# Gate tiles of the SwiGLUs in pairs: seven block products in place of eight

## The chip, the cores and the metric

The kernel runs on one core of one Trainium2 chip. The metric is the device time of one execution in microseconds. Five engines work side by side, each on its own queue of instructions: TensorE (matmuls, PE in the profile, with its weight loads shown apart as PEld), VectorE (DVE), ScalarE (ACT), GpSimd (POOL) and SyncE (SP), which issues most of the DMA transfers. A time is the slowest core's, and here there is one core.

## The reference

Two layers of an encoder act on 512 tokens of width 1024. A layer is a SwiGLU, a mixer (two attentions, a pooling branch, gates, an output map) and a second SwiGLU, each behind an RMS norm with shift and scale, each added to x under a gate. Shift, scale and gate come from a vector c through `w_ada`. The change touches the SwiGLU alone, of which the program runs four:

```
def swiglu(h, w_gate, w_up, w_down):
    return (jax.nn.silu(h @ w_gate) * (h @ w_up)) @ w_down
...
h = modulate(rms_norm(x, norm_gain[l, 0]), mod[:, 0], mod[:, 1])
x = x + 0.5 * mod[:, 2][:, None, :] * swiglu(h, ffn_w_gate[l, 0], ffn_w_up[l, 0], ffn_w_down[l, 0])
```

`w_gate` and `w_up` are 1024 x 2816, `w_down` is 2816 x 1024, all in float32.

## The kernel before

**Layout.** Features lie on the 128 partitions, tokens along the free dimension. The normed input h is held as eight blocks of 128 channels x 512 tokens. 2816 hidden features are 22 tiles of 128.

**Precision.** A float32 matmul is made of three matmuls in the faster type float32r. Each operand is split into a high half, the value rounded to float32r by ScalarE, and a low half, the rest, by VectorE (`split_to`, line 369; for weights `wchunk`, lines 268 and 270). `triple` (lines 117 to 122) issues high x high, high x low and low x high into one PSUM accumulation. So h lives in SBUF as `hhi` and `hlo`, and every weight block that comes from DRAM costs one ScalarE cast (L268) and one VectorE subtraction (L270).

**A SwiGLU** (`Ffn.run`, line 461). The 22 tiles are worked in two parts, of 12 and 10. For each tile, `gate_up` loads the gate and the up weights (512 KB each, eight blocks of 128 x 128), `unit` runs 8 x 3 matmuls of 512 columns for each into a PSUM bank, and `act` (line 452) makes silu of the gate on ScalarE (L454), the product on VectorE (L456) and its two halves (L370, L371). When the tiles of a part are done, `k_outer` (line 374) runs the down projection over this part's tiles: chunks of two tiles x 512 output channels, first for channels 0 to 511, then for the others. The first chunks are used as they come; the last two, or three, are held so that each of four output tiles ends by itself. `residual_tail` (line 416, L420) adds each output tile to x. The last part's second half is worked by halves of 256 tokens, so that the next phase's norm can begin on the first half.

**The beginning of a SwiGLU.** The very first one starts from `start` (line 523), which works three tiles while the norm is made. The others take tiles 0 and 1 by halves of the tokens behind the two halves of the norm (`Norm.back_start`, L357 to L360: scale, high half with shift, low half).

**Modulation rows.** The 144 rows of `w_ada` (512 KB each) are loaded and reduced on VectorE (`mod_step`, L194 and L197) as a side work: in the SwiGLUs each weight chunk adds `MOD_RATE`, here 1.0, to a credit, and each whole credit is one row. Rows go into the tag "v2", which has four buffers, as long as a SwiGLU is not in its last down stage.

**Buffers.** Tags of the SBUF pool that matter here, each a set of equal buffers that its tiles share: "b" with 17 blocks of 128 x 1024 (the products of a part, two halves each in one block), "v2" with 4, "raw" with 2 (weights as loaded), "whi" and "wlo" with 3 each, "ptb" with 2 (double size), "strip" with 2. In PSUM, "acc" and "mm" have four banks each; a bank holds 128 x 512.

**Order.** The program text is in the order of priority, and the Tile layer sets each engine's order of instructions from it: an instruction whose buffer or operand is not due yet can be passed by later ones of its engine. On the chip each engine works its list in order. Work off TensorE's path is placed by `later(delay, fn)` (line 98): it runs once the planned TensorE time, counted in 512-column matmuls in `pe[0]`, has gone on by `delay`. `issue_after` keeps some instructions behind others by hand, such as a modulation row's load behind the last weight load.

Of the kernel before, what the change touches and what calls it, by code (L numbers as in the profile page):

```python
# [15 lines left out]
F32 = mybir.dt.float32  # L16
F32R = mybir.dt.float32r
# [23 lines left out]
def encoder_kernel(tc, xT, c, w_ada, b_ada, gains, w_gate, w_up, w_down, w_qkv, w_f, w_ubg,  # L41
# [72 lines left out]
            t.run()  # L114
        polling[0] = False

    def triple(o, lh, ll, rh, rl, start, stop):
        poll()
        mm(o, lh, rh, start=start, stop=False)  # L119
        mm(o, lh, rl, start=False, stop=False)  # L120
        mm(o, ll, rh, start=False, stop=stop)  # L121
        pe[0] += 3.0 * max(o.shape[-1], 256) / T


# [98 lines left out]
        while mod_ptr[0] < min(len(mod_queue), (l * 9 + j + 1) * 8 - 16):  # L223
            mod_pop()

    MOD_RATE = 1.0
    in_ffn = [True]
    lo_share = [0, 0]

# [10 lines left out]
        else:  # L240
            yield

    def wchunk(src, shape, side=True, spare=None, lo_eng=None):
        if lo_eng is None:
            lo_share[1] += 1
            lo_eng = nc.gpsimd if lo_share[0] and lo_share[1] % lo_share[0] == 0 else nc.vector
        if quiet[0] > 0:
            quiet[0] -= 1
            if quiet[0] == 0:
                gate.clear()  # L250
        elif side and in_ffn[0] and mod_tag[0] == "v2":
            mod_credit[0] += MOD_RATE
            while mod_credit[0] >= 1.0:
                mod_credit[0] -= 1.0
                mod_pop()
        raw = st([P] + list(shape), F32, *(("b", NB) if spare else ("raw", NRAW)))
        last["dma"] = nc.sync.dma_start(raw, src).ins
        if spare == "ptb":
            both = st([P, 2] + list(shape), F32R, "ptb", 2)
            hi, lo = both[:, 0], both[:, 1]  # L260
        elif spare == "b":
            hi = st([P] + list(shape), F32R, "b", NB)
            lo = st([P] + list(shape), F32R, "b", NB)
        else:
            hi = st([P] + list(shape), F32R, "whi", 3)
            lo = st([P] + list(shape), F32R, "wlo", 3)
        with behind("scalar"):
            nc.scalar.copy(hi, raw)  # L268
        with behind("vector"):
            lo_eng.tensor_tensor(lo, raw, hi.bitcast(F32), op=ALU.subtract)  # L270
        return hi, lo
# [22 lines left out]
    class Norm:  # L294


        def __init__(self, l, s, xtag):
            self.l, self.s, self.xtag = l, s, xtag
            self.ssum = st([P, T], F32, "ssum", 1)
            self.xa = [None] * 4  # L300
            self.work = [None, None]
            self.state = [0, 0]
            self.pieces = [[], []]

        def sq(self, d, hs):

# [37 lines left out]
        def back_start(self, hs, bank):  # L344
            if self.state[hs] > 1:
                return
            self.front(hs, bank)
            self.state[hs] = 2
            w = self.work[hs]
            rb = bank((P, HALF))  # L350
            mm(rb, ones, w[:, HALF:2 * HALF], start=True, stop=True)  # L351
            cols = slice(hs * HALF, (hs + 1) * HALF)

            def piece(d):
                b = modc[:, self.l, 3 * self.s, d:d + 1]
                t = self.xa[d // 2][:, d % 2, cols]
                nc.vector.tensor_tensor(t, rb, t, op=ALU.mult)  # L357
                hi = hhi[:, d, cols]
                a_ins = nc.scalar.activation(hi, t, AF.Identity, bias=b)
                v_ins = nc.vector.scalar_tensor_tensor(hlo[:, d, cols], t, b, hi.bitcast(F32),  # L360
                                                       op0=ALU.add, op1=ALU.subtract)
                gate["scalar"], gate["vector"] = a_ins.ins, v_ins.ins
                last["norm"] = v_ins.ins

            self.pieces[hs] = [lambda d=d: piece(d) for d in range(KD)]
# [5 lines left out]
        lo_eng.tensor_tensor(lo, src, hi.bitcast(F32), op=ALU.subtract)  # L371


    def k_outer(chunk_src, nch, lhs_rhs, before_last=None):

        if before_last is None:
            parts, nheld = [(None, slice(0, T), [acc() for _ in range(4)])], 2
# [12 lines left out]

        held = []
        for c in range(nch):
            if before_last is not None:
                if c == nch - 2:
                    quiet[0] = 8
                    before_last()
                quiet[0] = 8
            hi, lo = wchunk(chunk_src(c), (2, T))  # L400
            if c < nch - nheld:
                for part in parts:
                    for j in range(4):
                        go(part, j, [(c, hi, lo)])
            else:
                held.append((c, hi, lo))
        if before_last is not None:
# [19 lines left out]
    FRONT, BACK, FRONT1, BACK1 = 8, 24, 16, 28  # L427
    FRONT2, BACK2 = 16, 28
    STEP = 3


    class Ffn:
# [19 lines left out]
        def act(self, n, pg, pu):  # L452
            sg = t1(T)
            nc.scalar.activation(sg, pg, AF.Silu)  # L454
            pr = t2(T)
            nc.vector.tensor_tensor(pr, pu, sg, op=ALU.mult)  # L456
            a = blk("b")
            split_to(a[:, 0, :], a[:, 1, :], pr)
            return a

        def run(self, nxt):
            l, s, ms = self.l, self.s, self.ms
            in_ffn[0] = True
            mod_tag[0] = "v2"
            for part, (f0, nf) in enumerate(((0, 12), (12, 10))):
                acts = []
                n = 0
                if part == 0 and self.norm is None:
                    acts = self.start()
                    n = 3  # L470
                elif part == 0:
                    g0, u0, g1 = self.pre
                    pg, pu, pg1 = mmt(), mmt(), mmt()
                    for hs in range(2):
# [14 lines left out]
                    n = 2  # L489
# [8 lines left out]
                mod_need(l, 3 * ms + 2)  # L498
                for c0 in (0, T):
# [8 lines left out]
                    last = part == 1  # L508
# [4 lines left out]
                    hook = None  # L513
                    if split:
                        hook = nxt.prefetch_weights if nxt is not None else (lambda: None)
                    for j, hs, o in k_outer(src, nf // 2, ops, hook):
                        d = c0 // P + j
                        residual_tail(d, hs, o, modc[:, l, 3 * ms + 2, d:d + 1], nxt if last else None)
                        if last and nxt is None:
                            cols = slice(0, T) if hs is None else slice(hs * HALF, (hs + 1) * HALF)  # L520
                            nc.sync.dma_start(out[:, d, cols], xd(d)[:, cols])

        def start(self):

# [566 lines left out]
```

## Time and profile before

| | us |
|---|---|
| median of 3 runs | 2472.27 (2471.41 to 2472.57) |
| the profiled execution | 2472.68 |
| its span in the profile | 2470.9 |

| engine | busy us | share of the span | instructions |
|---|---|---|---|
| TensorE matmuls (PE) | 2424.9 | 98% | 11898 |
| TensorE weight loads (PEld) | 2028.9 | 82% | 11898 |
| VectorE (DVE) | 1328.2 | 54% | 2362 |
| ScalarE (ACT) | 981.6 | 40% | 1634 |
| GpSimd (POOL) | 377.3 | 15% | 439 |

The page gives busy time by engine, the span in slices, the chain of work that ended last, the costliest groups of instructions and the DMA issues. Groups name the line of the kernel, the engine, the operation and its tiles, then the busy time, the mean of one in ns, and the idle time ahead of them with what ended it. Matmuls overlap in the records: one of 512 columns is recorded with 389 ns, but the next starts well before that has passed. So the price of a matmul is read from the distance of starts, not from its record.

The SwiGLUs lie at about 0 to 385, 882 to 1245, 1245 to 1615 and 2105 to 2471 us: a mixer lies after the first and after the third. The PE clock was granted at 0.998 on the mean.

### The profile page before, as it was taken

Reading aid. Unit: us, or ns where it says so; the run is one execution under the profiler, and the core shown is the slowest. Engines: PE = TensorE matmul, PEld = TensorE weight load, DVE = VectorE, ACT = ScalarE, POOL = GpSimd, SP = SyncE. Lnnn points to the kernel's source line nnn. Section 1 sums busy time; section 2 is a strip of 40 time slices with the busy share of each in tenths; the row PEclk is TensorE's granted clock in tenths of the full one; section 3 lists DMA queues with packets and bytes.
Section 4 is the critical chain, followed back from the end, with each engine's and each line's share of the span. In section 5 each row is a group of like instructions: output and inputs, shape, how many; then the busy total and the mean of one; then the engine's idle time right before and its main releaser. Section 6 shows DMA issues by size and latency. Waiting matters only on the chain. (4 is left out here: it accounts for less than half of the span.)

```text
span 2470.9 us, 31073 instructions
## 1 busy us (share of the span) xinstructions
PE 2424.9 (98%) x11898; PEld 2028.9 (82%) x11898; DVE 1328.2 (54%) x2362; ACT 981.6 (40%) x1634; POOL 377.3 (15%) x439
## 2 busy tenths in 40 slices
PE   7999999999999999999999999999999999999999
PEld 5888888777888898888898888978778888888888
DVE  8655536777643465555365533376766434533332
ACT  5322235676632342222342222366765323422221
POOL 2000012144432200000100000123354322000000
PEclk9999999999999999999999999999999999999999
DMA  7655542323333435565335533333233233233322
GB/s 276 222 194 189 195 136 87 87 72 98 104 97 104 150 101 201 173 209 182 120 118 189 189 118 94 128 92 92 67 108 101 86 119 128 77 94 101 95 94 94
DMA packets 116264, 320.03 MB, mean 130 GB/s; under 512 B 11122, under 2 KB 13298, under 8 KB 116116
## 3 DMA queue, kind: packets, MB, share of 16 engines
q1 hardware_dynamic: 114962, 313.86, 38.8%
q0 software_dynamic: 1152, 4.19, 0.4%
q8 instruction: 93, 1.52, 0.3%
q14 instruction: 55, 0.45, 0.1%
q10 hardware_dynamic: 2, 0.00, 0.0%
HBM read 311.64 MB, written 6.38 MB: 129 GB/s over the span
## 5 line engine op out<-in xcount | busy, mean ns | idle before, releaser
L268 ACT CAST whi<-raw 128x1024 fp32r<-128x1024 f32 (+1 forms) x395 | 412.1, 1046 | 1072.7 <-PE acc L120 398.0
L270 DVE TENSOR_TENSOR wlo<-raw,whi 128x1024 fp32r<-128x1024 f32 x387 | 478.7, 1239 | 527.2 <-ACT whi L268 514.7
L121 PE MATMUL mm<-hhi,wlo 128*128 128x512 f32 x1304 | 507.4, 389 | 0.4 <-DVE wlo L270 0.4
L119 PE MATMUL mm<-hhi,whi 128*128 128x512 f32 x1304 | 507.6, 389 | 0.0
L120 PE MATMUL mm<-hlo,whi 128*128 128x512 f32 x1304 | 507.3, 389 | 0.0
L119 PE MATMUL acc<-b,whi 128*128 128x512 f32 (+1 forms) x960 | 356.3, 371 | 0.0
L120 PE MATMUL acc<-b,whi 128*128 128x512 f32 (+1 forms) x960 | 354.6, 369 | 0.0
L121 PE MATMUL acc<-b,wlo 128*128 128x512 f32 (+1 forms) x960 | 354.5, 369 | 0.0
L121 PEld LDWEIGHTS mm<-hhi,wlo 128*128 128x128 f32 x1304 | 244.8, 188 | 51.8 <-DVE wlo L270 0.9
L120 PEld LDWEIGHTS mm<-hlo,whi 128*128 128x128 f32 x1304 | 244.8, 188 | 50.8
L119 PEld LDWEIGHTS mm<-hhi,whi 128*128 128x128 f32 x1304 | 245.1, 188 | 50.5
L197 DVE CUSTOM_DVE_ANT_0 v<-v,b,badac 128x1024 f32<-128x1024 f32 x144 | 189.6, 1318 | 37.1 <-DMA v<-in_w_ada_dram 36.8
L121 PEld LDWEIGHTS acc<-b,wlo 128*128 128x128 f32 x960 | 181.7, 189 | 29.8
L120 PEld LDWEIGHTS acc<-b,whi 128*128 128x128 f32 x960 | 181.5, 189 | 29.6 <-POOL b L371 0.4
L119 PEld LDWEIGHTS acc<-b,whi 128*128 128x128 f32 x960 | 181.2, 189 | 28.6
L119 PE MATMUL acc<-hhi,whi 128*128 128x512 f32 x480 | 190.7, 399 | 1.7 <-ACT hhi L558 1.7
L120 PE MATMUL acc<-hlo,whi 128*128 128x512 f32 x480 | 188.2, 392 | 0.8 <-DVE hlo L561 0.8
L121 PE MATMUL acc<-hhi,wlo 128*128 128x512 f32 x480 | 188.6, 393 | 0.0
L456 DVE TENSOR_TENSOR t<-mm,t 128x512 f32<-128x512 f32 x86 | 59.5, 692 | 203.4 <-PE mm L121 202.4
L119 PE MATMUL acc<-whi,hhi 128*128 128x512 f32 x336 | 137.8, 411 | 4.1 <-ACT t L648 3.7
L121 PE MATMUL acc<-whi,hlo 128*128 128x512 f32 x336 | 132.1, 393 | 0.0
L120 PE MATMUL acc<-wlo,hhi 128*128 128x512 f32 x336 | 131.7, 392 | 0.0
(233 smaller groups left out, 3348.1 us busy)
## 6 DMA issues: line engine op xcount, KB each, us to landing
v<-in_w_ada_dram SPq DMA_DIRECT2D x144, 512.0 KB, 4.6
raw<-in_w_down_dram SPq DMA_DIRECT2D x88, 512.0 KB, 3.8
raw<-in_w_up_dram SPq DMA_DIRECT2D x82, 512.0 KB, 3.6
raw<-in_w_gate_dram SPq DMA_DIRECT2D x79, 512.0 KB, 3.7
raw<-in_w_ubg_dram SPq DMA_DIRECT2D x56, 512.0 KB, 3.6
raw<-in_w_qkv_dram SPq DMA_DIRECT2D x42, 512.0 KB, 3.8
raw<-in_w_branch_dram SPq DMA_DIRECT2D x24, 512.0 KB, 3.7
raw<-in_w_out_dram SPq DMA_DIRECT2D x16, 512.0 KB, 3.7
```

Source lines behind the costliest of these rows:

```text
L119: mm(o, lh, rh, start=start, stop=False)
L120: mm(o, lh, rl, start=False, stop=False)
L121: mm(o, ll, rh, start=False, stop=stop)
L197: dot = nc.vector.tensor_tensor_reduce(out=raw, in0=raw, in1=silc[0], scale=1.0, scalar=badac[:, l, j, d:d + 1], op0=ALU.mult, op1=ALU.add ...
L268: nc.scalar.copy(hi, raw)
L270: lo_eng.tensor_tensor(lo, raw, hi.bitcast(F32), op=ALU.subtract)
L456: nc.vector.tensor_tensor(pr, pu, sg, op=ALU.mult)
```

## The change

The gate product of two neighbouring tiles is a 2 x 2 block matrix times a 2 x 2 block matrix: two tiles of features by two halves of the channels (four blocks of 128 each), times two halves of the channels by two halves of the tokens (256 each). The plain way takes eight block products. The new `pair` takes seven, in the form of Strassen and Winograd, on sums of blocks:

- `block_sums` makes four sums or differences of blocks of h, once in a SwiGLU, and splits each in high and low halves. They stay in "b" (seven blocks, and one in "pta") to the end of the SwiGLU. With a norm they are made from the scaled input, and the shift enters as a bias; in the first SwiGLU they are made from `hhi` + `hlo`. Eight or twelve steps are spread with `later`, 8 matmuls apart.
- `pair_weights` loads the two gate tiles raw into "b", makes the sums of weight blocks on VectorE, and splits all in halves, in four steps. The halves go to "ptb" (two buffers), "v2" (two) and "strip" (two), one raw sum to "v2" for a while.
- `pair` runs the seven products, each 4 x 3 matmuls of 256 columns. Two of the four "acc" banks are accumulated on after ScalarE has copied them (`kept`), which gives the partial sums that several outputs share.
- `gate_up_pair` adds the parts into a "v2" block (`put_gate`, VectorE), makes silu there, and runs the two up tiles as before; between their matmuls it places the four steps of the next pair's weights.
- Plain tiles remain: six in the first SwiGLU, four in the others (`plain`). So there are 8 pairs in the first and 9 in each other one, 35 in all.
- A SwiGLU has four parts, of 6, 6, 4 and 6 tiles, each with its down stage. The two halves of the channels of a down stage use "acc" and then "mm" banks, and in the second half the next part's first pair weights are made (`then`).
- `product` keeps gate x up in the PSUM bank of the up tile, and both halves are split from there. Before, it went to SBUF.
- `MOD_RATE` is 1.5, since the gate weights of pairs no longer go through `wchunk`. `u1`, the second up tile's weights at the start of a SwiGLU, is loaded after the first half of the norm, not after both.

The diff, cut to its core:

```
-    MOD_RATE = 1.0
+    MOD_RATE = 1.5
...
-    def k_outer(chunk_src, nch, lhs_rhs, before_last=None):
+    def k_outer(chunk_src, nch, lhs_rhs, before_last=None, bank=None, then=None):
...
+    PARTS = (6, 6, 4, 6)
...
-            pr = t2(T)
-            nc.vector.tensor_tensor(pr, pu, sg, op=ALU.mult)
+            return self.product(pu, sg)
+
+        def product(self, pu, sg):
+
+            nc.vector.tensor_tensor(pu, pu, sg, op=ALU.mult)
             a = blk("b")
-            split_to(a[:, 0, :], a[:, 1, :], pr)
+            split_to(a[:, 0, :], a[:, 1, :], pu)
             return a
...
+        def block_sums(self, norm):
...
+            work = [] if norm is not None else [lambda i=i: whole(i) for i in range(4)]
+            work += [lambda: both(3, 3, 1, ALU.subtract), lambda: both(1, 1, 2, ALU.subtract), lambda: split(1),
+                     lambda: both(2, 3, 2, ALU.add), lambda: split(2), lambda: both(4, 4, 2, ALU.subtract),
+                     lambda: split(4), lambda: split(3)]
+            for i, z in enumerate(work):
+                later(8 * i, z)
...
+        def pair_weights(self, n):
...
+            def sums():
+                split_to(*d[0], r[0])
+                g(s3, a11, a21, op=ALU.subtract)
+                g(a21, a21, a22, op=ALU.add)
+
+            def more():
+                g(r3[:, 0], a21, a11, op=ALU.subtract)
+                g(r3[:, 1], a12, r3[:, 0], op=ALU.subtract)
+                split_to(*d[2], r3)
+
+            steps = [sums, lambda: split_to(*d[1], r[1]), more, lambda: split_to(*e, s3)]
...
+        def pair(self, w, put, bank):
...
+            x = bank()
+            prod(x, "a11", (0, h1), True, True)
+            c1 = t2(T)
+            a = kept(x, c1[:, :HALF])
+            y = bank()
+            prod(y, "a12", (4, h1), True, True)
+            put(0, h1, y, a)
+            v = bank()
+            prod(v, "s1", 1, True, True)
+            e = kept(v, c1[:, HALF:])
+            prod(x, "s2", 2, False, True)
+            c2 = t2(T)
+            b = kept(x, c2[:, :HALF])
+            z = bank()
+            prod(z, "a22", 4, True, True)
+            prod(v, "s4", (4, h2), False, True)
+            put(0, h2, v, b)
+            prod(x, "s3", 3, False, True)
+            c = kept(x, c2[:, HALF:])
+            put(1, h1, z, c)
+            put(1, h2, x, e)
...
+        def gate_up_pair(self, n, more):
+
+            us = [self.gate_up(1, n + f) for f in range(2)]
+            g = blk("v2", F32)
...
+            self.pair(self.ready, put_gate, acc)
+            self.ready, steps = self.next_pair(n + 2, more)
+            for f in range(2):
+                pu = mmt()
+                for k in range(KD):
+                    self.unit(pu, us[f], ks=(k,))
+                    if k in (1, 5) and steps:
+                        steps.pop(0)()
+                acts.append(self.product(pu, g[:, f, :]))
+            return acts
...
-                    u1 = self.gate_up(1, 1)
+                        if hs == 0:
+                            u1 = self.gate_up(1, 1)
...
+                    acts += self.plain((2, 3), self.norm)
...
-                    g = self.gate_up(0, f0 + n)
-                    u = self.gate_up(1, f0 + n)
-                    pg, pu = mmt(), mmt()
-                    self.unit(pg, g)
-                    self.unit(pu, u)
-                    acts.append(self.act(n, pg, pu))
-                    n += 1
+                    acts += self.gate_up_pair(f0 + n, n + 2 < nf)
+                    n += 2
```

More of the change, by code (lines that the diff above doesn't have):

```diff
@@ L251, in wchunk @@
         elif side and in_ffn[0] and mod_tag[0] == "v2":
[L252 to L256, printed above, removed]
+            side_work(MOD_RATE)
+        raw = st([P] + list(shape), F32, *(home or (("b", NB) if spare else ("raw", NRAW))))
         last["dma"] = nc.sync.dma_start(raw, src).ins
@@ L406, in k_outer @@
                 held.append((c, hi, lo))
+        if then is not None:
+            then()
         if before_last is not None:
@@ new lines, in pair, with prod, kept @@
+        def pair(self, w, put, bank):
+            thi, tlo = self.sums
+            h1, h2 = slice(0, HALF), slice(HALF, T)
+            def prod(o, a, b, start, stop):
+                wh, wl = w[a]
+                for k in range(4):
+                    if isinstance(b, int):
+                        rh, rl = thi[b][:, k, :], tlo[b][:, k, :]
+                    else:
+                        rh, rl = (z[:, b[0] + k, b[1]] for z in (hhi, hlo))
+                    triple(o[:, :HALF], wh[:, k, :], wl[:, k, :], rh, rl, start and k == 0, stop and k == 3,
+                           onto=not start)
+            def kept(o, where):
+                nc.scalar.copy(where, o[:, :HALF])
+                return where
+            x = bank()
[19 more added lines that the diff above has]
+            put(1, h2, x, e)
@@ new lines, in plain, with next_pair @@
+        def plain(self, tiles, norm):
+            made = []
+            for i, n in enumerate(tiles):
+                g, u = self.gate_up(0, n), self.gate_up(1, n)
+                if i == (norm is None):
+                    self.block_sums(norm)
+                pg, pu = mmt(), mmt()
+                self.unit(pg, g)
+                self.unit(pu, u)
+                made.append(self.act(n, pg, pu))
+            return made
+        def next_pair(self, n, more):
+            return self.pair_weights(n) if more else (None, [])
@@ L512, in run, with then @@
                     split = last and c0 > 0
[L513 removed]
+                    hook, then = None, None
                     if split:
                         hook = nxt.prefetch_weights if nxt is not None else (lambda: None)
[L516 removed]
+                    elif c0 > 0:
+                        def then(n=f0 + nf):
+                            self.ready, steps = self.next_pair(n, not last)
+                            for i, z in enumerate(steps):
+                                later(8 * i, z)
+                    for j, hs, o in k_outer(src, nf // 2, ops, hook, acc if c0 == 0 else mmt, then):
                         d = c0 // P + j
```

93 lines of the change are left out of this document (83 added, 10 removed).

## The prediction

> **What bounds the kernel now.** I read the page's first rows, then the busy time by stretches of 62 us, then TensorE's own waits, then the timeline for the cadence of the matmuls.
>
> ```profile
> span 2470.9 us, 31073 instructions
> PE 2424.9 (98%) x11898; PEld 2028.9 (82%) x11898; DVE 1328.2 (54%) x2362; ACT 981.6 (40%) x1634; POOL 377.3 (15%) x439
> ...
> 124.00:186.00 62.00, 62.00 (x275) 51.36 (x274) 35.75 (x55) 14.81 (x18) 0.00 (x0) 1.00 0.56 190
> 558.00:620.00 62.00, 57.23 (x302) 44.72 (x301) 44.45 (x123) 43.25 (x103) 31.17 (x45) 0.97 0.34 105
> 992.00:1054.00 62.00, 62.00 (x275) 51.38 (x274) 34.04 (x52) 15.28 (x17) 0.00 (x0) 1.00 0.56 190
> 2232.00:2294.00 62.00, 62.00 (x275) 51.38 (x274) 18.82 (x18) 13.43 (x14) 0.00 (x0) 1.00 0.30 94
> ...
> PE mm L121 <- DVE wlo L270: 0.4, 1, 0.4
> ```
>
> In the stretches (columns: PE, PEld, DVE, ACT, POOL, clock, DMA share, GB/s) the SwiGLUs, three of the four shown, keep TensorE busy for all 62 us at full clock. Its idle time lies in the attention (558 to 620) and the start. The only wait of TensorE on a feed-forward weight is 0.4 us. So in the SwiGLUs time is matmuls, one for one, and VectorE has 42% free where modulation rows are still being reduced (35.75 busy of 62) and 70% where they are not (18.82). Busy time can't price a matmul, since records overlap; the cadence can:
>
> ```profile
> 2139.54 0.69 DVE L456 TENSOR_TENSOR t<-mm,t 128x512 f32<-128x512 f32 x1 [3.39 <-PE mm L121]
> 2140.37 1.23 DVE L270 TENSOR_TENSOR wlo<-raw,whi 128x1024 fp32r<-128x1024 f32 x1
> 2141.51 0.69 DVE L371 TENSOR_TENSOR b<-t,b 128x512 fp32r<-128x512 f32 x1
> 2150.42 0.69 DVE L456 TENSOR_TENSOR t<-mm,t 128x512 f32<-128x512 f32 x1 [3.38 <-PE mm L121]
> ...
> 2092.72 0.48 DVE L420 SCALAR_TENSOR_TENSOR xv<-mm,modc,xv 128x256 f32<-128x256 f32 x1 [0.96 <-PE mm L121]
> 2094.16 0.48 DVE L420 SCALAR_TENSOR_TENSOR xv<-mm,modc,xv 128x256 f32<-128x256 f32 x1 [0.96 <-PE mm L121]
> ...
> L119 PEld LDWEIGHTS mm<-hhi,whi 128*128 128x128 f32 x1304 | 245.1, 188 | 50.5
> ```
>
> Each L456 waits for the end of one feature tile, gate and up, 2 x 8 x 3 = 48 matmuls of 512 columns: 2150.42 - 2139.54 = 10.88 us, **226.7 ns** each. Each L420 on a half of the tokens waits for 2 chunks x 2 x 3 = 12 matmuls of 256 columns, each with weights of its own: 1.44 us, **120 ns** each.
>
> **The change, part by part.**
>
> *Seven products for eight.* Two gate tiles were 2 x 8 x 3 = 48 matmuls of 512: 10.88 us. They become 7 products x 4 blocks x 3 = 84 of 256: 84 x 0.120 = 10.08 us. The first SwiGLU has 22 tiles with 6 plain, 8 pairs; the other three have 4 plain, 9 pairs: 35 pairs x 0.80 = **-28.0 us**. TensorE's clock and everything else on TensorE stay.
>
> Two rules of the Trainium skill bear on this. The page "TensorE: Matmul & The Clock Gate", section "Back-to-back issue gap", gives N/2.4 + 2.5 ns, 215.8 and 109.2 ns, an estimate of -1.19 us a pair or -41.5 us in all; both cadences here are some 11 ns longer, so the measurement decides for 28.0. The same page's "The mechanism" (under packing small matmuls) says that a weight load overlaps running matmuls only when its row group differs, which speaks against 36 more loads a pair; the rows disagree (a last rival, below).
>
> *VectorE.* Its prices:
>
> ```profile
> L270 DVE TENSOR_TENSOR wlo<-raw,whi 128x1024 fp32r<-128x1024 f32 x387 | 478.7, 1239 | 527.2 <-ACT whi L268 514.7
> L197 DVE CUSTOM_DVE_ANT_0 v<-v,b,badac 128x1024 f32<-128x1024 f32 x144 | 189.6, 1318 | 37.1 <-DMA v<-in_w_ada_dram 36.8
> L371 DVE TENSOR_TENSOR b<-t,b 128x512 fp32r<-128x512 f32 x88 | 60.2, 685 | 2.8 <-ACT b L370 2.8
> L456 DVE TENSOR_TENSOR t<-mm,t 128x512 f32<-128x512 f32 x86 | 59.5, 692 | 203.4 <-PE mm L121 202.4 <-ACT t L454 1.0
> L420 DVE SCALAR_TENSOR_TENSOR xv<-acc,modc,xv 128x512 f32<-128x512 f32 x56 | 42.0, 749 | 58.0 <-PE acc L121 58.0
> L360 DVE SCALAR_TENSOR_TENSOR hlo<-b,modc,hhi 128x256 fp32r<-128x256 f32 x32 | 14.0, 483 | 0.5 <-ACT hhi L359 0.5
> L357 DVE TENSOR_TENSOR b<-mm,b 128x256 f32<-128x256 f32 x16 | 6.0, 418 | 0.0
> L197 DVE DVE_READ_ACCUMULATOR2_ANT modc<- 128x1 f32 x144 | 11.9, 83 | 0.0
> ...
> L268 ACT CAST whi<-raw 128x1024 fp32r<-128x1024 f32 x387 | 405.5, 1051 | 1070.4 <-PE acc L120 398.0 <-PE mm L120 338.2 <-issue 271.3
> L454 ACT ACTIVATE t<-mm 128x512 f32<-128x512 f32 x86 | 51.0, 593 | 1.9 <-PE mm L121 1.8
> L798 ACT CAST pta<-mm 128x256 fp32r<-128x256 f32 x32 | 12.0, 374 | 6.6 <-PE mm L794 6.0
> ```
>
> The weights of a pair cost three low halves of 1024 (3.72), one of 512 (0.69) and four sums of 512 (2.76): 7.2 us, where two plain gate tiles cost 2.48. The four additions of `put_gate` are 4 x 0.42 = 1.7. For a part of six tiles TensorE takes 3 x (10.08 + 10.88) + 144 x 0.2267 = 95.5 us. VectorE takes 6 up and 6 down low halves 14.9, weights 21.5, `put_gate` 5.0, products and their low halves 6 x 1.38 = 8.3, residual 8 x 0.75 = 6.0: 55.6 us, 58%; with 12 chunks x 1.5 = 18 modulation rows at 1.40, 80.9 us, **85%**. The same sum for before is 59.1 of 97.9, 60%, against 35.75 of 62 measured, so the method holds. ScalarE: 21 casts x 1.05, 3 of 512, 12 copies x 0.37, 6 silu, 6 casts: 35 us of 95, no bound.
>
> Both fit, but not evenly: behind the pair's products, in the 10.88 us of its up tiles, VectorE has the next weights 7.2, two `put_gate` 0.8, one product 1.4, one low half 1.2 and up to three modulation rows 4.2, 14.8 us in all. The 3.9 us over run into the next pair, whose third product starts 2 x 12 x 0.12 = 2.9 us in, its fourth (`s2`) after 4.3 and its last (`s3`) after 8.6, and whose own ten microseconds ask VectorE for only 3.5. So late weights are mostly covered; bound 0 to 1.4 us (one modulation row ahead of `a11`) a pair while rows remain. I take 0.15, since the deadlines are staggered. Which pairs these are:
>
> ```profile
> 124.00:186.00 62.00, 14.98 (x23) 1.00 0.56 190
> 1054.00:1116.00 62.00, 15.37 (x25) 1.00 0.56 196
> 1364.00:1426.00 62.00, 15.45 (x24) 1.00 0.56 191
> 1426.00:1488.00 62.00, 1.29 (x2) 1.00 0.33 107
> ```
>
> These are L197 alone: the first two SwiGLUs and half of the third, 8 + 9 + 5 = 22 pairs: **+3.3 us** (0 to 31).
>
> *Opening of a SwiGLU with a norm.* The block sums cost VectorE eight operations of 512 (5.5), four low halves of 512 (2.7) and eight of 256 with bias (3.9): 12.1 us.
>
> ```profile
> 882.57 0.28 PE L119 MATMUL mm<-hhi,ptb 128*128 128x256 f32 x1
> ...
> 896.04 0.89 DVE L360 SCALAR_TENSOR_TENSOR hlo<-b,modc,hhi 128x256 fp32r<-128x256 f32 x2 [0.25 <-ACT hhi L359]
> ```
>
> The second SwiGLU starts at 882.57, has 4 plain tiles, 43.5 us, and reaches its first pair at 926. VectorE is free of the norm at 896.9: 29.2 us for sums 12.1, products 5.5, seven low halves 8.7, weights 7.2: 33.5, and 46 with nine modulation rows. 4 to 17 us are over; but `a11`, `a12`, `s1` and the first sum alone are due at once, and nothing needs those rows. `u1`'s load, moved between the norm's halves, adds at most its 1.24 there. Bound 0 to 17, I take 1.2 for each of three: **+3.6**. The first SwiGLU's sums (16 us) lie behind three plain tiles (33 us): 0.
>
> *Shorter parts.* Sixteen more residual operations a SwiGLU (8 a part, four parts) are in the 85%. The four-tile part reads its last product in the tenth matmul of the down stage, 9 x 0.2267 = 2.04 us after the last up matmul; from product to low half the rows above took 2141.51 + 0.69 - 2139.54 = 2.66 us with another operation between, 1.96 without: 0 to 2.0 us with a modulation row ahead, take 0.4. Its second half of channels has only 2.72 us between a free weight buffer and the use of its second chunk, for 1.05 + 1.24: 0 to 1.2, take 0.2. The last part's split stage has three chunks, not five, so its third has about 1 us of slack, where two L420 fit: 0 to 1.5, take 0.5. Four SwiGLUs: **+4.4** (0 to 19). Six-tile parts have 24 matmuls, 5.4 us, ahead of held chunks: 0.
>
> *The rest.* DMA carries the same bytes. The product left in PSUM is the same operation as L456. `kept` has one or two products, 1.4 to 2.9 us, for a 0.37 us copy: 0.
>
> Sum against the profiled execution's own 2472.7 (span 2470.9 and 1.8 outside; the median shown is 2472.3, 0.4 lower): 2472.7 - 28.0 + 3.3 + 3.6 + 4.4 = **2456.0 us**.
>
> **Rivals.**
>
> *Full gain.* If every wait above is covered: 2472.7 - 28.0 = 2444.7. For it: TensorE lost 0.4 us in all feed-forward weights before. Against: VectorE goes from 60 to 85%, and attention, at 44.45 of 62, loses 4.8 us a stretch.
>
> *The opening backlog is paid in full.* 17 us in the second SwiGLU, 10 in the third (half its rows), 4 in the fourth: 31 - 28.0 + 3.3 = 6 over at most, 1 to 3 if a part is covered: about 2474, no change. For it: 46 us of work in 29. Against: rows and late sums can wait.
>
> *Four buffers of tag "v2"; slower.* A pair holds two for `s2`, `s4`, one for `r3`, one for the gate; modulation rows use the same four.
>
> ```profile
> v<-in_w_ada_dram SPq DMA_DIRECT2D x144, 512.0 KB, 4.6
> raw<-in_w_gate_dram SPq DMA_DIRECT2D x79, 512.0 KB, 3.7
> ```
>
> A row holds one for 4.6 + 1.4 = 6.0 us. The third step of the next weights is due 30 matmuls, 6.8 us, into the up tiles, takes 3.7 and has 4.7 us of slack to `s2`: one row in its way stalls TensorE by 1.3 us, two in turn by 7.3, and the up weights on SP's queue are behind the row's load. With 22 pairs it turns the change into a loss from 28.0/22 = 1.3 us a pair; at 2.0 a pair it is 2472.7 - 28.0 + 8.0 + 44 = 2497. Against: three rows in 21 us need 18 buffer-microseconds, and of 4 x 21 = 84 the pair itself holds about 2 x 13 for `s2`/`s4`, 19 for the gate and 4 for `r3`: 35 are free.
>
> *Exposed weight loads.* If the 36 added loads of a pair cost their 188 ns, 35 x 36 x 0.188 = 237 us: 2682. The 256-column rows, with a load per matmul, exclude it.
>
> **How the numbers follow.** Forecast 0.46, full gain 0.24, backlog 0.13, buffers 0.16, loads 0.01. A measurement here can tell 0.2%, 4.9 us. Both first cases are faster: 0.70; backlog is the same: 0.13; the last two slower: 0.17. The likeliest case's own range is 2447 to 2466; the range given runs from just below full gain, 2443, to just past the backlog, 2476, and leaves out the slower cases.
>
> **What would show it.** TensorE: 35 x 84 more matmuls of 256 columns at 120 ns, 35 x 48 fewer of 512. VectorE near 52 of 62 us in the first SwiGLU. Waits of TensorE on block sums or weight sums of 10 to 15 us in total, at openings and the four-tile part. Waits over 1.3 us a pair, ScalarE's cast of `v2` behind L197, mean the buffers; a cadence above 130 ns in pairs would make the whole gain wrong.

## The result, and the profile after

| us | median | range | runs |
|---|---|---|---|
| before, timed beside the change | 2471.84 | 2470.59 to 2472.57 | 4 |
| after | 2450.07 | 2449.19 to 2451.09 | 4 |

The ratio is **0.9913** (95% interval 0.9901 to 0.9925): 21.8 us faster, where 16.3 us were forecast (2472.3 to 2456.0). The profiled execution after took 2450.88 us.

The first rows of the page of after, to be held against those of before:

```profile
span 2448.9 us, 34028 instructions
PE 2396.8 (98%) x12966; PEld 2051.8 (84%) x12966; DVE 1600.5 (65%) x2859; ACT 1110.3 (45%) x1888; POOL 377.3 (15%) x439
```

VectorE went from 1328 to 1600 us of work, and TensorE from 11898 to 12966 records: more, but smaller, matmuls. The 1068 more are 35 x 36 = 1260 for the pairs, less 192: the last part, whose second half is worked by halves of the tokens, has six tiles in place of ten, and so 48 matmuls fewer in each SwiGLU. Where the time went is seen by phases. This is the timeline of TensorE after, at the first matmul of the second, third and fourth SwiGLU (883.05, 1239.52, 2091.19) and around one pair:

```profile
883.05 0.28 PE L119 MATMUL mm<-hhi,ptb 128*128 128x256 f32 x1
...
1077.61 0.28 PE L119 MATMUL acc<-hhi,ptb 128*128 128x256 f32 x1
...
1087.58 0.39 PE L119 MATMUL mm<-hhi,whi 128*128 128x512 f32 x1
...
1098.49 0.28 PE L119 MATMUL acc<-hhi,ptb 128*128 128x256 f32 x1
...
1239.52 0.28 PE L119 MATMUL mm<-hhi,ptb 128*128 128x256 f32 x1
...
2091.19 0.28 PE L119 MATMUL mm<-hhi,ptb 128*128 128x256 f32 x1
```

and the same first matmuls before (that of the second SwiGLU, 882.57, is quoted in the prediction):

```profile
1245.76 0.28 PE L119 MATMUL mm<-hhi,ptb 128*128 128x256 f32 x1
...
2104.89 0.28 PE L119 MATMUL mm<-hhi,ptb 128*128 128x256 f32 x1
```

From such starts and the ends of the spans the phases follow. The forecast by SwiGLU adds the prediction's own terms: its pairs at -0.80, its rows, its opening, and 1.1 for its parts.

| phase | before us | after us | difference | forecast |
|---|---|---|---|---|
| first SwiGLU | 365.6 | 366.5 | **+1.0** | -4.1 |
| second SwiGLU | 363.2 | 356.5 | -6.7 | -3.6 |
| third SwiGLU | 363.2 | 355.3 | -7.9 | -4.2 |
| fourth SwiGLU | 366.0 | 357.7 | -8.3 | -4.9 |
| both mixers | 991.4 | 991.2 | -0.2 | 0 |

Three SwiGLUs gained about twice what was forecast; the first gained nothing. **The pairs.** The 84 matmuls of the pair above took 1087.58 - 1077.61 = 9.97 us, 118.7 ns each, and its two up tiles 1098.49 - 1087.58 = 10.91 us. So a pair saves 10.88 - 9.97 = 0.91 us, nine of them 8.2: nearly all that the last two SwiGLUs gained. **The first SwiGLU** has eight pairs, 7.3 us, and is 1.0 longer: 8.3 us were lost. The waits of TensorE after on feed-forward work show the place:

```profile
PE acc L121 <- DVE wlo L273: 3.5, 1, 3.5
...
PE acc L119 <- ACT b L378: 1.7, 2, 0.9
```

One wait of 3.5 us stands out: a down stage ("acc" from "b") waits for the low half of its weights. Here is TensorE's timeline of after at that place:

```profile
93.23 0.39 PE L120 MATMUL acc<-b,whi 128*128 128x512 f32 x1
97.09 0.80 PE L121 MATMUL acc<-b,wlo 128*128 128x512 f32 x1 [3.47 <-DVE wlo L273]
97.68 0.63 PE L119 MATMUL acc<-b,whi 128*128 128x512 f32 x1
98.11 0.63 PE L120 MATMUL acc<-b,whi 128*128 128x512 f32 x1
```

It is the first down stage of the first SwiGLU. Behind the wait matmuls start 98.11 - 97.68 = 0.43 us apart, where 0.227 is usual. The busy time by stretches tells the same (columns: PE, PEld, DVE, ACT, POOL, clock, DMA share, GB/s), here 8 us from 94 on and 62 us stretches in the first, second and fourth SwiGLU:

```profile
94.00:102.00 8.00, 4.91 (x12) 3.85 (x13) 7.96 (x13) 2.58 (x3) 0.00 (x0) 0.60 0.62 211
...
62.00:124.00 62.00, 58.25 (x245) 47.24 (x244) 61.39 (x93) 23.25 (x30) 0.00 (x0) 0.94 0.69 245
124.00:186.00 62.00, 61.87 (x393) 56.13 (x392) 45.52 (x77) 22.92 (x36) 0.00 (x0) 1.00 0.53 180
186.00:248.00 62.00, 62.00 (x319) 53.15 (x318) 50.46 (x76) 22.52 (x28) 0.00 (x0) 1.00 0.59 200
992.00:1054.00 62.00, 61.93 (x354) 54.49 (x353) 47.40 (x76) 22.99 (x35) 0.00 (x0) 1.00 0.58 201
2232.00:2294.00 62.00, 62.00 (x350) 54.48 (x349) 32.68 (x42) 20.55 (x28) 0.00 (x0) 1.00 0.33 111
```

Twelve matmuls ran in the 4.91 us behind the wait, at a granted clock of 0.60 over the stretch; at 0.227 it would have been 21, so the slow clock cost some 2.2 us more within the stretch, and 2.6 until the usual pace is back at 102.63. And **VectorE was full**: 61.39 of 62 us. In the stretches that follow it has 11 to 17 us free. What it did, in the timeline of after (the cast is the high half of the first down chunk, on ScalarE; the low half is the last row):

```profile
84.89 1.05 ACT L271 CAST whi<-raw 128x1024 fp32r<-128x1024 f32 x1 [1.16 <-DMA raw<-in_w_down_dram]
...
86.19 1.28 DVE L379 TENSOR_TENSOR b<-b,b 128x512 fp32r<-128x512 f32 x2
87.39 1.89 DVE L499 TENSOR_TENSOR b<-b,b 128x512 f32<-128x512 f32 x3
...
94.02 1.27 DVE L197 CUSTOM_DVE_ANT_0 v<-v,b,badac 128x1024 f32<-128x1024 f32 x1
...
95.22 0.68 DVE L379 TENSOR_TENSOR b<-mm,b 128x512 fp32r<-128x512 f32 x1
95.82 1.21 DVE L273 TENSOR_TENSOR wlo<-raw,whi 128x1024 fp32r<-128x1024 f32 x1
```

The high half is there at 85.94 (84.89 + 1.05), the low half starts at 95.82. Between them VectorE's list has block sums (L499), their low halves (L379), a product with its low half and a modulation row, without a gap. The low half waits for no transfer there: what holds it up is its place in the list.

The stretch of 34 us ahead of the stall, before the change:

```profile
60.00:94.00 34.00, 34.00 (x151) 28.15 (x151) 26.13 (x42) 11.30 (x14) 0.00 (x0) 1.00 0.71 247
```

VectorE was busy for 26.1 of 34 us there, so 7.9 us were free. Into these the change put 15.0 us of sums, by these groups of after in the same stretch (4.6 + 3.9 + 3.8 + 1.4 + 1.3):

```profile
L495 DVE TENSOR_TENSOR b<-hhi,hlo 128x1024 f32<-128x1024 f32 x4 | 4.6, 1218 | 0.0
L379 DVE TENSOR_TENSOR b<-b,b 128x512 fp32r<-128x512 f32 x6 | 3.9, 680 | 0.0
L499 DVE TENSOR_TENSOR b<-b,b 128x512 f32<-128x512 f32 x6 | 3.8, 681 | 0.0
...
L379 DVE TENSOR_TENSOR b<-b,pta 128x512 fp32r<-128x512 f32 x2 | 1.4, 680 | 0.0
L499 DVE TENSOR_TENSOR b<-b 128x512 f32<-128x512 f32 x2 | 1.3, 682 | 0.0
```

### The profile page after: what moved, and what is told of

It reads as the page before. It is cut to its first block, busy times and chain, and to the rows that moved or that the text cites. A ratio compares the mean times of both kernels' runs of the same rounds, so it can differ in the third digit from the quotient of the medians.

```text
span 2448.9 us, 34028 instructions
## 1 busy us (share of the span) xinstructions
PE 2396.8 (98%) x12966; PEld 2051.8 (84%) x12966; DVE 1600.5 (65%) x2859; ACT 1110.3 (45%) x1888; POOL 377.3 (15%) x439
## 5 line engine op out<-in xcount | busy, mean ns | idle before, releaser
L121 PE MATMUL mm<-hhi,wlo 128*128 128x512 f32 x744 | 289.8, 390 | 0.7 <-DVE wlo L273 0.4
L119 PE MATMUL mm<-hhi,whi 128*128 128x512 f32 x744 | 290.2, 390 | 0.0
L120 PE MATMUL mm<-hlo,whi 128*128 128x512 f32 x744 | 290.0, 390 | 0.0
L119 PE MATMUL acc<-b,whi 128*128 128x512 f32 (+1 forms) x704 | 264.1, 376 | 1.7 <-ACT b L378 1.7
L120 PE MATMUL acc<-b,whi 128*128 128x512 f32 (+1 forms) x704 | 262.4, 373 | 0.0
L121 PEld LDWEIGHTS mm<-hhi,wlo 128*128 128x128 f32 x744 | 139.7, 188 | 30.9 <-DVE wlo L273 1.6
L119 PEld LDWEIGHTS mm<-hhi,whi 128*128 128x128 f32 x744 | 140.0, 188 | 27.9
L120 PEld LDWEIGHTS mm<-hlo,whi 128*128 128x128 f32 x744 | 139.7, 188 | 27.4
L119 PEld LDWEIGHTS acc<-b,whi 128*128 128x128 f32 x704 | 133.3, 190 | 23.8 <-ACT b L378 2.6
L120 PEld LDWEIGHTS acc<-b,whi 128*128 128x128 f32 x704 | 133.3, 189 | 23.2 <-DVE b L379 0.9
L120 PE MATMUL mm<-b,whi 128*128 128x512 f32 (+1 forms) x384 | 135.8, 354 | 0.0
L119 PE MATMUL mm<-b,whi 128*128 128x512 f32 (+1 forms) x384 | 135.8, 354 | 0.0
L121 PE MATMUL mm<-b,wlo 128*128 128x512 f32 (+1 forms) x384 | 135.6, 354 | 0.0
```

The lines of the kernel that those rows point to most:

```text
L119: mm(o, lh, rh, start=start, stop=False, skip_group_check=onto)
L120: mm(o, lh, rl, start=False, stop=False, skip_group_check=onto)
L121: mm(o, ll, rh, start=False, stop=stop, skip_group_check=onto)
```

## The experiments

Theory A: the block sums of the first SwiGLU crowd VectorE, and the stall at its first down stage is the loss. Against it stood that the shorter parts or the raised rate of modulation rows make the loss, and that the pairs are not bound by TensorE at all. (Where an expectation calls the late weights those of the second down chunk: by the order of casts and low halves they are the first's.) The times of before that stand beside the runs are 2471.50, 2472.08 and 2473.11 us.

**1. The sums on GpSimd.**

```diff
-            op = nc.vector.tensor_tensor
+            op = (nc.vector if norm is not None else nc.gpsimd).tensor_tensor
```

> Edit: in the first SwiGLU alone the twelve additions and subtractions of block_sums (four of 1024 columns, eight of 512) run on GpSimd in place of VectorE; the splits stay. Theory A (VectorE's backlog): in the changed kernel VectorE is busy without a gap from 62 to 102 us, so the low half of the down stage's second chunk starts 4.4 us after its high half, TensorE waits 3.5 us at 93.2 and then runs some 5 us at a lower granted clock. Taking 4.6 + 5.1 = 9.7 us off VectorE there removes both: the first SwiGLU gets 6 us shorter, about 2444 us in all. Theory B (the DMA queue): the wait comes from the down weights' load, which stands on SP's queue between modulation rows; then the sums' engine is of no matter and the time stays within 1.5 us of 2450.

2449.95 us (2447.26 to 2450.43), 0.9911 [0.9897, 0.9924]: no gain over the change. TensorE now waited 3.2 us at 68.25 for a modulation coefficient and 1.1 at the down stage. VectorE's timeline in this run:

```profile
65.92 2.27 DVE L273 TENSOR_TENSOR wlo<-raw,whi 128x1024 fp32r<-128x1024 f32 x1
...
68.18 2.24 DVE L197 CUSTOM_DVE_ANT_0 v<-v,b,badac 128x1024 f32<-128x1024 f32 x1
...
79.26 0.69 DVE L470 TENSOR_TENSOR mm<-mm,t 128x512 f32<-128x512 f32 x1
...
86.21 1.21 DVE L273 TENSOR_TENSOR wlo<-raw,whi 128x1024 fp32r<-128x1024 f32 x1
```

and GpSimd's:

```profile
64.86 4.47 POOL L499 TENSOR_TENSOR b<-b,b 128x512 f32<-128x512 f32 x2
```

While GpSimd works on the sums, a low half takes VectorE 2.27 us, and 1.21 once they are done; a row 2.24 instead of 1.27. Two sums on GpSimd take 4.47, 2.24 each, and the operations of the two engines start in turn; what a sum takes there with VectorE idle, no run shows. So each sum taken from VectorE (0.68 us) cost it about 1.0 us on the operation beside it. The product, with one operand in PSUM, kept its 0.69. The Trainium skill, page "SBUF — State Buffer", section "Who interferes with whom", states this: a VectorE instruction with two SBUF inputs and a GpSimd one that reads SBUF lock each other out. The trace agrees. The edit therefore took little work off VectorE, moved most of the wait to another place, and decides nothing on theory A.

**2. The shorter parts alone** (all tiles plain, rows at the rate of before).

```diff
-    MOD_RATE = 1.5
+    MOD_RATE = 1.0
...
-            return self.pair_weights(n) if more else (None, [])
+            return None, []
...
-                    acts += self.gate_up_pair(f0 + n, n + 2 < nf)
+                    acts += self.plain((f0 + n, f0 + n + 1), None)
```

(and no `block_sums`.)

> Edit: the parts of 6, 6, 4, 6, the banks of the down stage and the product in PSUM as in the change, but all tiles plain, no block sums, MOD_RATE 1.0 as before. Theory A: the short parts cost only the waits seen at the four-tile part (0.9 and 0.8 us where rows are reduced, 0 where not): 1 to 3 us over before, 2473 to 2475. Then the pairs alone are worth 23 to 25 us. Rival: shorter parts cost 4.4 us or more (16 more residual operations a SwiGLU, less cover at the split stage), 2476 or more.

2470.73 us (2469.74 to 2471.37), 0.9996 [0.9987, 1.0005], below what either side gave. **Four parts in place of two cost nothing on balance**, with the product left in PSUM. The row of busy times of its page shows why it is a balance:

```profile
PE 2422.7 (98%) x11706; PEld 2017.5 (82%) x11706; DVE 1369.6 (55%) x2426; ACT 976.6 (40%) x1634; POOL 375.9 (15%) x439
```

These are the 192 matmuls fewer: 384 of 256 columns went and 192 of 512 came. At the prediction's 120 and 226.7 ns that is an estimate of 2.6 us saved, behind which the shorter parts can hide a cost of 1 to 2 us. The pairs with all they bring are the difference that is left.

**3. Parts of 6, 8 and 8.**

```diff
-    PARTS = (6, 6, 4, 6)
+    PARTS = (6, 8, 8)
```

> Edit: the changed kernel with parts of 6, 8, 8 in place of 6, 6, 4, 6: no four-tile part, three down stages a SwiGLU. Theory A: the two waits at the four-tile part (0.9 and 0.8 us and their slow starts, 1.9 together) go, nothing else: 2447 to 2449. Rival: with eight products, seven block sums and two raw blocks the 17 blocks of tag b are short, the next pair's weights come late at each part's end and TensorE waits there: above 2452.

2452.72 us (2450.00 to 2453.80), 0.9922 [0.9910, 0.9935]: no gain. The waits at the four-tile part are gone, the stall of 3.45 us at 96.89 is not, and pairs wait for `kept` copies (L570), up to 1.2 us where in the change it was 0.1. The time is the one of the rival, but the waits are not on the next pair's weights, as the rival had it; why the copies come late stays open.

```profile
PE acc L121 <- DVE wlo L273: 4.2, 2, 3.4
PE acc L119 <- ACT t L570: 3.2, 4, 1.2
```

**4. Both of the last.**

```diff
-    PARTS = (6, 6, 4, 6)
+    PARTS = (6, 8, 8)
...
-            op = nc.vector.tensor_tensor
+            op = (nc.vector if norm is not None else nc.gpsimd).tensor_tensor
```

> Edit: both edits, sums of the first SwiGLU on GpSimd and parts of 6, 8, 8. If the two losses are independent the gains add: 2442 to 2443 us, near the 2440 that 35 pairs of 0.91 us would give. If the buffers of tag b are short, it is slower than the one with GpSimd alone.

2450.35 us (2449.19 to 2453.24), 0.9916 [0.9903, 0.9930]. Two edits that gain nothing alone gain nothing together; the wait at 67.5 is again there, with 3.16 us.

**5. No sums in the first SwiGLU.** This kernel leaves out the sums of blocks of h there: the halves are made from the high half of h alone, so the gate values of its pairs are others.

```diff
...
-            work = [] if norm is not None else [lambda i=i: whole(i) for i in range(4)]
-            work += [lambda: both(3, 3, 1, ALU.subtract), lambda: both(1, 1, 2, ALU.subtract), lambda: split(1),
+            work = [lambda: both(3, 3, 1, ALU.subtract), lambda: both(1, 1, 2, ALU.subtract), lambda: split(1),
...
-                later(8 * i, z)
+                if norm is not None or i in (2, 4, 6, 7):
+                    later(8 * i if norm is not None else 8 * (i + 4), z)
```

> Edit: in the first SwiGLU the twelve additions and subtractions of block_sums are left out; the splits are made of blocks of the high half of h where the sums would be, so that SwiGLU's pairs compute other values. Nothing takes the work over, so GpSimd stays idle there. Theory A (VectorE's backlog): 9.7 us fewer on VectorE between 73 and 91 us, and the wait of 3.5 us with its slow matmuls (6 us together) goes: 2443 to 2445. Theory B (the down weights' load on SP's queue): the wait stays, the time is within 1.5 us of 2450.

2444.30 us (2442.97 to 2445.29), 0.9887 [0.9874, 0.9901]. The first SwiGLU takes 359.0 us, 7.5 less; the wait is gone, and with it the slow clock:

```profile
94.00:102.00 8.00, 8.00 (x37) 6.60 (x37) 7.63 (x11) 1.32 (x2) 0.00 (x0) 1.00 1.01 385
```

Thirty-seven matmuls in these 8 us, not twelve. This is theory A.

**6. Are the modulation rows to blame?** One row a chunk in the first part of the first SwiGLU alone.

```diff
+    first_rate = [1.0]
...
-            side_work(MOD_RATE)
+            side_work(first_rate[0])
...
+                first_rate[0] = MOD_RATE
```

> Edit: the changed kernel with a rate of 1.0 modulation rows a chunk in place of 1.5 in the first part of the first SwiGLU alone, 1.5 after. Eight rows must stand before the first down stage in either case, so about four rows (5.6 us of VectorE) move out of the stretch from 62 to 105 us. Theory A: the wait of 3.5 us shrinks to under 1 us and the slow matmuls behind it go, 2444 to 2446. Theory B: the rows' loads leave SP's queue as well, so the time falls as much; this run tells whether a better version is there, not A from B.

2451.52 us (2449.37 to 2452.70), 0.9917 [0.9903, 0.9930]: no gain. Rows that a phase needs by its end come in a burst there if the rate has not brought them in. VectorE's timeline of this run:

```profile
90.88 1.29 DVE L197 CUSTOM_DVE_ANT_0 v<-v,b,badac 128x1024 f32<-128x1024 f32 x1
...
92.74 1.28 DVE L197 CUSTOM_DVE_ANT_0 v<-v,b,badac 128x1024 f32<-128x1024 f32 x1
...
94.61 1.28 DVE L197 CUSTOM_DVE_ANT_0 v<-v,b,badac 128x1024 f32<-128x1024 f32 x1
...
95.81 1.23 DVE L274 TENSOR_TENSOR wlo<-raw,whi 128x1024 fp32r<-128x1024 f32 x1
```

The low half of the first down chunk (L274 here) starts at 95.81 as in the change: the sums before it end some 2.5 us earlier, but three rows stand behind them where one stood. TensorE waited 4.06 us.

**7. The rate of before everywhere.**

```diff
-    MOD_RATE = 1.5
+    MOD_RATE = 1.0
```

> Edit: MOD_RATE 1.0 in all SwiGLUs, so that rows go on into later ones. Theory A: the first SwiGLU loses its wait as with the lower rate in its first part, the waits of 0.8 to 0.9 us at the four-tile parts of the first two SwiGLUs go too, since fewer rows stand in the way: 2442 to 2446. Rival: the rows that are due before a mixer or a down stage come in a burst and cost as much there: 2449 or more.

2463.69 us (2461.06 to 2464.62), 0.9964 [0.9951, 0.9976]. The stall stays (4.1 us), and the first mixer takes 507.8 us for 494.8: eight rows (10.55 us of VectorE) fall into 80 us near its end (800 to 880), where there are none at 1.5, and TensorE waits once for long, for a weight that ScalarE casts late because its load came late:

```profile
PE acc L119 <- ACT whi L271: 10.7, 1, 10.7
```

So the rival holds, and the raised rate belongs to the change: with fewer chunks to earn credit, it keeps the rows ahead of their due times.

**8. Eight products for seven.** The a22 product is run twice, so the gate values are others; everything beside TensorE stays.

```diff
+            prod(z, "a22", 4, False, True)
```

> Edit: each pair runs one product (a22 with the fourth sum) a second time into the same bank, so that there are eight again, on the same operands and with the same sums; the gate's values are then others. If TensorE alone bounds the pairs, 35 x 12 matmuls x 118.7 ns = 49.9 us are added: 2500. If VectorE bounds some of them, its work hides behind the added product and less is added: below 2492.

2502.04 us (2499.06 to 2503.46), 1.0119 [1.0106, 1.0133]: 52.0 us more than the change, 1.49 us a pair for twelve matmuls of 118.7 ns, 1.42. **TensorE bounds the pairs**, and what VectorE and ScalarE do for them is covered: had those set the pace, the added product would have cost less than its own time.

**9. The rival of the four "v2" buffers, provoked.** Twice the rate of rows.

```diff
-    MOD_RATE = 1.5
+    MOD_RATE = 3.0
```

> Edit: MOD_RATE 3.0 in place of 1.5, so rows are done earlier and their density doubles: some six rows a pair, 8.4 us more of VectorE in 21 us where 18.3 are used, and three more buffers of tag v2 asked for in each pair. The prediction's rival (v2 buffers, or VectorE) would show here if it is real at all: waits of TensorE at the pairs of the first SwiGLU, ScalarE's casts into v2 waiting for L197, by 2 us or more a pair for some 14 pairs, 2475 or more. If pairs bear it, only the start gets worse: 2450 to 2460.

2493.30 us (2492.24 to 2495.03), 1.0084 [1.0069, 1.0099]: slower than before. The first SwiGLU takes 402.3 us, 35.7 more. SP's queue between 62 and 400 us in this run:

```profile
SPq L194 <- DVE modc L197: 78.2, 42, 8.1
SPq L194 <- DVE mm L470: 62.8, 7, 13.5
```

and after:

```profile
SPq L194 <- DVE v L601: 45.6, 7, 11.3
SPq L194 <- DVE modc L197: 39.2, 15, 4.5
```

SP's queue waits with a row's load (L194) for a "v2" buffer, and the weights queued behind it come late. ScalarE in this run, in the same window:

```profile
ACT whi L271 <- DMA raw<-in_w_down_dram: 61.6, 8, 20.2
```

Down weights kept ScalarE waiting for 61.6 us in eight places. The mechanism of the rival is real, at twice the rate; at 1.5 SP waits too, but no matmul waits for it. Most of the time is lost at down stages and plain tiles, and not in the pairs, as the rival had it: four of the first SwiGLU's pairs took 10.4 to 11.3 us in place of 9.97, some 3.5 us together.

**10. Rows behind the first down chunks.** Half a row a chunk in the first part, and the rows due then are placed behind three chunks of the down stage.

```diff
+    first_rate = [0.5]
...
-            side_work(MOD_RATE)
+            side_work(first_rate[0])
...
-                mod_need(l, 3 * ms + 2)
+                first = part == 0 and self.norm is None
+                if not first:
+                    mod_need(l, 3 * ms + 2)
...
+                    if first and c0 == 0:
+                        def then():
+                            mod_need(l, 3 * ms + 2)
+                            first_rate[0] = MOD_RATE
```

> Edit: in the first part of the first SwiGLU a rate of 0.5 rows a chunk, and the rows that are due before the residual are traced behind the first half's three down chunks, not ahead of them; 1.5 after that. Eight to nine rows (12 us of VectorE) leave the stretch from 62 to 97 us or stand behind the low halves that TensorE waits for; 56 rows still come in this SwiGLU where 48 are due by the mixer's end. Theory A (VectorE's list holds rows and sums ahead of the low half): the wait of 3.5 us and the slow matmuls go, first SwiGLU 359 to 361 us in place of 366.5, 2444 to 2446 in all, as where the sums were left out, and this one computes the whole reference. If the wait stays, its place in the list was not the rows'.

2447.82 us (2447.78 to 2448.84), 0.9901 [0.9884, 0.9917]: the first SwiGLU takes 361.9 us, 4.6 less, with waits of 0.4 to 0.8 us left. That is short of the 2444 to 2446 expected, but the long wait and the slow matmuls are gone: taking its other work out of VectorE's way helps too.

**11. The sums further apart.** One number: the steps of the first SwiGLU's sums are 14 matmuls apart.

```diff
-                later(8 * i, z)
+                later((8 if norm is not None else 14) * i, z)
```

> Edit: the twelve steps of the first SwiGLU's block sums 14 matmuls apart in place of 8; nothing else. The last then comes about 109 us in, 21 us ahead of the first pair. Theory A: fewer of the sums stand ahead of the down chunks' low halves, so the wait shrinks to 0 to 2 us, 2444 to 2448; as VectorE is busy to 124 us whatever the order, some of it may come back as late weights of the first pair at 130 us. Theory B: no change.

**2445.30 us** (2442.15 to 2446.95), **0.9888** [0.9873, 0.9902]: the lowest median of the versions that compute all of the reference. The first SwiGLU takes 359.0 us, what it takes without the sums. Its stretches:

```profile
62.00:94.00 32.00, 31.75 (x141) 25.97 (x139) 32.00 (x50) 12.51 (x19) 0.00 (x0) 1.00 0.73 257
...
94.00:102.00 8.00, 8.00 (x37) 6.64 (x36) 8.00 (x14) 3.40 (x6) 0.00 (x0) 1.00 0.66 235
```

and its timeline of the cast of the first down chunk and of VectorE:

```profile
82.72 1.05 ACT L271 CAST whi<-raw 128x1024 fp32r<-128x1024 f32 x1
...
88.71 1.23 DVE L273 TENSOR_TENSOR wlo<-raw,whi 128x1024 fp32r<-128x1024 f32 x1
89.84 1.30 DVE L499 TENSOR_TENSOR b<-b,b 128x512 f32<-128x512 f32 x2
...
99.34 1.30 DVE L499 TENSOR_TENSOR b<-b,b 128x512 f32<-128x512 f32 x2
```

VectorE is as full as before, 32.00 of 32 us, but the low half now starts at 88.71 and is done at 89.94, 2.2 us ahead of the first matmul that reads it (92.18), and the last sums stand behind it. Not the amount of VectorE's work cost the time, but what stood ahead of the down weights. This kernel and the change were each timed against the kernel before, not against one another, and their intervals touch (0.9902 and 0.9901); the 7.5 us of the first SwiGLU are read from the two profiles.

## Why the prediction was right, and where not

- **TensorE bounds the pairs, and time is matmuls: right** (experiment 8; experiment 2 shows that the gain is theirs). The term was mis-sized: -28.0 came from 120 ns in the down stage by halves; in the pairs the cadence is 118.7 ns, 9.97 us a pair, 35 x 0.91 = -31.9. The prediction's estimate of -41.5 by the Trainium skill (page "TensorE: Matmul & The Clock Gate", section "Back-to-back issue gap") is further off; the page gives that formula for a single matmul by itself, and the 118.7 ns decide.
- **Rows in the pairs, +3.3:** too much. Of the 32 pairs whose 84 matmuls run without others between them, 30 took 9.97 us and two about 0.35 us longer (10.31 and 10.36 us): +0.7. The upper bound of 31 was never near.
- **Openings with a norm, +3.6:** nothing. TensorE's waits list none on block sums in these three SwiGLUs.
- **Shorter parts, +4.4:** experiment 2 puts them at nothing, on balance, without pairs. The prediction's "everything else on TensorE stay" leaves out the 192 matmuls fewer, an estimate of -2.6 us that the sum lacks. With pairs, the four-tile part waits 0.93 and 0.82 us for its last product in the first two SwiGLUs and not in the others: +1.7, against 1.6 forecast for that part alone. The split stage and the second half's chunk show no wait.
- **"The first SwiGLU's sums (16 us) lie behind three plain tiles (33 us): 0" is the step that failed.** It laid 15 us of sums against the length of the stretch, not against what VectorE had free in it, 7.9 us by a row that was there to be read. And it took the end of the sums as what is late, when the list sets them ahead of the down stage's weights. Price, by experiments 5 and 11: 7.5 us. Of it 3.5 are the wait and some 2.6 the slow clock; 0.9 more, at its four-tile part, is gone too in experiment 11, and the rest I can't lay to single waits.
- The sum thus came out 5.9 us too high (2456.0 for 2450.1): 11.3 us of costs were given where -31.9 needed some 10, and the pairs' term was 3.9 short. That the two totals of costs agree is chance: 11.3 was spread over four SwiGLUs, and some 8 of the measured 10, which are net of the matmuls saved in the last parts, lie in the first. Most of the costs forecast were not paid, and a stall that was put at nothing took their place: so far the nearness of the time is luck.
- **Full gain** fails mainly by that stall: with the sums spread, 2445.3 stands beside its 2444.7. That they meet is luck in part, since its -28.0 was too small: with -31.9 it would be 2440.8, and some waits are left in experiment 11. **The backlog** was the right mechanism in the wrong SwiGLU, the one for which it was put at nothing. **The buffers** don't bind at 1.5 rows a chunk and do at 3. **Exposed weight loads** are excluded by 118.7 ns with a weight load for each matmul.
- "VectorE near 52 of 62 us in the first SwiGLU": 61.4, then 45.5 and 50.5. The mean of the three is 52.5, and it hid the stretch that mattered. "Waits of TensorE on block sums or weight sums of 10 to 15 us in total": none on either. The 3.5 us are a wait on a down weight that stood behind block sums, and the 1.7 at the four-tile parts are on products.

What stays open: some 1.5 us of the second SwiGLU (6.7 gained of 8.2) are only in part in the waits listed, and why the list puts the down chunk's low half behind all the sums at 8 and ahead of the last of them at 14 was seen from its result alone.

## What to carry to other kernels

Work that is put behind matmuls must be laid against the free time of its engine in that very stretch, and then against the order of its list: what stands behind it, and which of that is due first. When a few microseconds of an off-path engine's work are moved, try first to space them otherwise; here one number gave a lower median than any change of engine, rate or tiling. Taking a small operation away from a full engine can hand the time back if, where it now runs, it slows that engine's other operations, as the sums on GpSimd did.

## What the runs showed of the hardware

**A wait costs more than itself.** After TensorE had waited 3.47 us, matmuls started 0.43 us apart, about half the usual pace, for about 5 us. Five other runs showed the same in their first SwiGLU for 3 to 5.5 us, behind single waits of 3.16 to 4.22 us; a wait of 3.18 us (experiment 1) left the clock at 1.00. The Trainium skill, page "TensorE: Matmul & The Clock Gate", section "Why this matters for your kernels", warns of idle gaps over some 3 us, and that the clock then falls to half: these traces agree, with 3.2 us on either side. But the length of one wait doesn't decide alone. In experiment 9 two waits of 2.17 and 2.04 us with two matmuls between them were followed by the same slow pace (63.52 to 69.07), and in the attention before the change the clock was 0.97 from 558 to 620 us, where no wait was longer than 1.1 us.

**GpSimd beside VectorE.** Operations of VectorE with two operands in SBUF and 1024 columns took 2.1 to 2.3 us beside GpSimd's sums of 512 columns instead of 1.21 to 1.27, while those sums took 2.24; a product with one operand in PSUM kept its 0.69.
